# One column copied by VectorE in place of ScalarE at the end of a convolution's odd half

## The chip, the cores and the metric

The kernel runs on one core of a Trainium2 chip. The core has a matrix engine (TensorE, PE in the profile), a vector engine (VectorE, DVE), a scalar engine (ScalarE, ACT), a third elementwise engine (GpSimd, POOL) and a queue engine that mainly issues DMAs (SyncE, SP); ACT issues some DMAs too. Each engine works through its own list of instructions in order. An instruction that needs another engine's result, or a DMA's, waits at the head of its list, and everything behind it on that engine waits with it.

The metric is the device time of one execution in microseconds (us). Lower is better.

## The reference

One block of a diffusion transformer, with 1024 latent tokens of width 1024 and 256 context tokens. A combined projection feeds a Conformer convolution branch and a grouped-query attention branch; the two are gated, added and projected again. All arithmetic is float32. What matters here is the convolution: 31 taps, each of the 1024 channels by itself.

```
def conv_module(u, gate, conv_w, conv_b, ln_g, ln_b, w_conv_out):
    a, g = jnp.split(u, 2, axis=-1)
    y = a * jax.nn.sigmoid(g)
    pad = CONV_KERNEL // 2
    y = lax.conv_general_dilated(
        y, conv_w[:, None, :], window_strides=(1,), padding=[(pad, pad)],
        dimension_numbers=('NWC', 'WIO', 'NWC'), feature_group_count=CONV_WIDTH) + conv_b
    y = jax.nn.silu(layer_norm(y, ln_g, ln_b))
    y = y * jax.nn.silu(gate)
    return y @ w_conv_out
```

## The kernel before

The 1024 channels of the convolution are done in eight blocks of 128 (j = 0 to 7), one after the other. A channel lies on a partition and the tokens lie along the row. The input of a block is split into even tokens (`E`, 512 columns) and odd tokens (`O`, 512 columns), both in one tile `y`; the two running sums lie in a PSUM tile of two banks, which the profile calls `pconv`. There is only one such tile, so a block starts only when the one ahead of it is done.

`conv_taps` puts the steps of a block on a list `taps` as small functions. `pump` takes the next ones from that list and issues them, between the matmuls of the projections (`filler`), which run at the same time. In order a block is: `first` (two ACT instructions fill the two sums), 15 taps on VectorE into the even sum, `even_end` (POOL adds `E` and `O`), 15 taps into the odd sum, `odd_end`, `evens`, `turn`, 15 more taps, and `last`, whose VectorE instruction is the last reader of `pconv`; POOL then adds the block's output to `ysum`, and SP stores it (`accD`).

`odd_end` is the place of the change. A VectorE instruction writes columns 0 to 510 of `O` from the input one column to the right and the odd sum. Column 511 has no neighbour to its right, and so it is copied from the odd sum by itself (line 809). `evens` begins with a small reduction of `edge` and then reads `O`, so its first large instruction (line 817) stands behind that copy.

After the eighth block the kernel gives the PSUM banks of the convolution to the attention (`unshare(2)`, `share({"o": 1})`, `share({"s": 5})`). The first matmuls of the attention, those of `max_pieces`, which find the row maxima of the scores, write tiles `ps` in these banks. VectorE reduces each to a maximum (`mx`).

The projections go through a stream of jobs (`stream`, `wparts`, `proj`): a weight half is loaded by SP (`wraw`), cast on ACT to its high part (`whi`), and subtracted on POOL or VectorE to its low part (`wlo`). 24 matmuls (`ppj`) make one half of a job, after which ACT empties the bank (`ts`). While the flag `held` is set, the instructions of VectorE, ACT, POOL and PE stay in the order of the program text; it is cleared for VectorE, ACT and POOL once the projections of queries, keys and values are issued, while the eighth block is still under way, and from there a scheduler orders these engines' lists (`urgent()` raises an instruction's priority in it). Helpers record all instructions on line 50, so the profile tells them apart by tile names, not by lines.

Of the kernel before, what the change touches and what calls it, by code (L numbers as in the profile page):

```python
# [34 lines left out]
def block_kernel(ctx: ExitStack, tc: tile.TileContext, x, cx, cc, wmod, bmodT, bmodg, vecs, gpost,  # L35
# [18 lines left out]
    PE, V, S, G = (Ordered(e) for e in (nc.tensor, nc.vector, nc.scalar, nc.gpsimd))  # L54
# [11 lines left out]
    def tl(tag, shape, bufs, dtype=F32, pool="sb"):  # L66
        return pools[pool].tile(list(shape), dtype, tag=tag, bufs=bufs, name=nm(tag))
# [13 lines left out]
    def share(bufs):  # L81
        p = tc.tile_pool(name=nm("share"), bufs=1, space=PSUM, reuse_waits="tile")
        shares.append((p, p.__enter__(), bufs))

    def unshare(n):
        for _ in range(n):
            shares.pop()[0].__exit__(None, None, None)

    def pt(tag, shape=(P, 512), dtype=F32):
        if not any(tag in bufs for _, _, bufs in shares):  # L90
            tag = "s"
        for _, pool, bufs in shares:
            if tag in bufs:
                return pool.tile(list(shape), dtype, tag=tag, bufs=bufs[tag], name=nm("p" + tag))
# [685 lines left out]
    def conv_taps(j, y):  # L780
        st = {}
        E, O = y[:, 0, :], y[:, 1, :]

        def first():
            if j == 0:
                unshare(1)
                share({"conv": 1})
            st["acc"] = pt("conv", (P, 2, 512))
            S.activation(st["acc"][:, 1, :], O, AF.Identity, scale=cw[:, j, 14:15])
            S.activation(st["acc"][:, 0, :], E, AF.Identity, scale=cw[:, j, 15:16])  # L790

        def even_end():

            G.tensor_tensor(out=E, in0=E, in1=O, op=ALU.add)
            st["edge"] = tl("edge", (P, 10), 2)

        def tap(c, src, k, w):
            o = k - 7
            a, b = max(0, -o), min(512, 512 - o)
            acc = st["acc"][:, c, a:b]  # L800
            V.scalar_tensor_tensor(out=acc, in0=src[:, a + o:b + o], scalar=w, in1=acc, op0=ALU.mult, op1=ALU.add)

        def odd_end():

            acc = st["acc"]
            V.tensor_tensor(out=st["edge"][:, 0:8], in0=O[:, 0:8], in1=cw[:, j, 16:31:2], op=ALU.mult)
            V.scalar_tensor_tensor(out=O[:, 0:511], in0=O[:, 1:512], scalar=cw[:, j, 16:17], in1=acc[:, 1, 0:511],
                                   op0=ALU.mult, op1=ALU.add)
            S.copy(O[:, 511:512], acc[:, 1, 511:512])

        def evens():
            acc = st["acc"]
            st["out"] = tl("acc", (P, T), 2)
            out = st["out"][:].rearrange("p (u r) -> p r u", r=2)
            edge = st["edge"]
            V.tensor_reduce(out=edge[:, 8:9], in_=edge[:, 0:8], axis=AX.X, op=ALU.add)
            V.scalar_tensor_tensor(out=out[:, 0, 1:512], in0=acc[:, 0, 1:512], scalar=cvb[:, j:j + 1],
                                   in1=O[:, 0:511], op0=ALU.add, op1=ALU.add)
            V.scalar_tensor_tensor(out=out[:, 0, 0:1], in0=acc[:, 0, 0:1], scalar=cvb[:, j:j + 1], in1=edge[:, 8:9],
                                   op0=ALU.add, op1=ALU.add)  # L820

        def turn():
            acc = st["acc"]
            V.scalar_tensor_tensor(out=acc[:, 0, :], in0=acc[:, 0, :], scalar=ncvb[:, j:j + 1], in1=O,
                                   op0=ALU.add, op1=ALU.add)

        def last():
            acc = st["acc"]
            out = st["out"]
            V.scalar_tensor_tensor(out=out[:].rearrange("p (u r) -> p r u", r=2)[:, 1, :], in0=E,  # L830
                                   scalar=cs[:, j, 16:17], in1=acc[:, 0, :], op0=ALU.mult, op1=ALU.subtract)
            if j == 0:
                G.tensor_copy(ysum[:], out[:])
            else:
                G.tensor_tensor(out=ysum[:], in0=ysum[:], in1=out[:], op=ALU.add)
            SP.dma_start(out=accD[j][:], in_=out[:])

        ks = [k for k in range(16) if k != 7]
        taps.append(first)
        taps.extend(lambda k=k: tap(0, E, k, cw[:, j, 2 * k + 1:2 * k + 2]) for k in ks[:-1])  # L840
        taps.append(lambda: (even_end(), tap(1, O, 0, cw[:, j, 0:1])))
        taps.extend(lambda k=k: tap(1, O, k, cw[:, j, 2 * k:2 * k + 1]) for k in ks[1:] if k != 8)
        taps.append(odd_end)
        taps.append(evens)
        taps.append(turn)
        taps.extend(lambda k=k: tap(0, E, k, cs[:, j, k:k + 1]) for k in ks)
        taps.append(last)
# [775 lines left out]
```

## Time and profile before

| what | value |
|---|---|
| median of 3 runs | 1400.5 us (1398.6 to 1407.2) |
| the profiled execution | 1406.56 us |
| its span, first to last instruction | 1404.8 us |
| PE busy | 1353.0 us, 96% of the span |
| DVE busy | 1022.3 us, 73% |
| POOL busy | 712.5 us, 51% |
| ACT busy | 564.3 us, 40% |

The convolution's taps run on DVE from 76 to 571 us of the span, beside the projections on PE; the attention follows, from 563 us on. All times in rows of the profile are us from the start of the span. In a row of the timeline the first number is the start, the second the duration, and the bracket at the end tells how long the engine had been idle before it and what ended that. In a row of the waits the numbers are the sum, the count and the longest. In a row of the windows the busy time of each engine stands with the number of instructions, then the clock granted to PE as a share of full speed, the busy share of the DMA engines and their GB/s.

### The profile page before, as it was taken

To read this page: it belongs to the slowest core of one execution; us is meant where nothing else is said; L and a number is where in the kernel's file an instruction comes from. 1 tells how busy PE (TensorE), PEld (TensorE's weight loads), DVE (VectorE), ACT (ScalarE), POOL (GpSimd) and SP (SyncE) were. 2 spreads that over 40 slices of the span, in tenths; PEclk is the share of its full clock that TensorE was granted. 3 is DMA by queue.
4 is the path that set the end of the run, shared out by engine and by line. 5 is a ranking of instruction groups with operands and counts; after the bars stand their busy time and mean duration, and the time that the engine had idled before them with its cause. 6 is when DMAs were issued, how large, how long until landed. Compare 5 with 4: busy or idle time off the path is not lost.

```text
span 1404.8 us, 19526 instructions
## 1 busy us (share of the span) xinstructions
PE 1353.0 (96%) x6520; PEld 1003.3 (71%) x6520; DVE 1022.3 (73%) x1513; ACT 564.3 (40%) x1397; POOL 712.5 (51%) x577
## 2 busy tenths in 40 slices
PE   5999999999999999799999999999999999999996
PEld 3767898988889888566666666566666565788874
DVE  3477988897989896757766676677676676349967
ACT  5542344435343432145444444454454444222332
POOL 1121346567666552256764655565456666263623
PEclk9999999999999999899999999999999999999998
DMA  9731533544534448414554444544365567699754
GB/s 320 266 124 46 184 119 131 191 133 141 176 125 156 140 159 224 143 61 140 176 166 121 136 145 141 165 136 153 97 191 163 209 213 259 204 317 341 257 182 153
DMA packets 153332, 242.45 MB, mean 173 GB/s; under 512 B 19936, under 2 KB 72716, under 8 KB 153232
## 3 DMA queue, kind: packets, MB, share of 16 engines
q1 hardware_dynamic: 139792, 218.07, 47.4%
q10 hardware_dynamic: 13440, 23.14, 5.8%
q8 instruction: 51, 0.84, 0.3%
q14 instruction: 49, 0.40, 0.1%
HBM read 161.50 MB, written 79.52 MB: 172 GB/s over the span
## 4 chain that ended last, share of the span: by engine, by line
PE 76%; DVE 9%; DMA 4%; ACT 3%; POOL 3%; issue 3%; ACTq 0%; SPq 0%; POOLq 0%; DVEq 0%
PE ppj L50 34%; PE po L50 21%; PE ps L50 17%; PE pm L50 4%; DVE pconv L50 3%; DVE t L50 2%; DMA wm<-in_wmod 1%; DVE mx L50 1%; DMA y<-in_wout 1%; ACT pe L50 1%; POOL y L50 1%; POOL wgl L50 1%; DMA r<-r1D 1%; ACTq L50 0%; DVE acc L50 0%
## 5 line engine op out<-in xcount | busy, mean ns | idle before, releaser
L50 PE MATMUL ppj<-t,whi 128*128 128x512 f32 x1728 | 617.7, 402 | 4.6 <-DVE t L50 2.6
L50 PEld LDWEIGHTS ppj<-t,whi 128*128 128x128 f32 x1728 | 328.1, 190 | 107.7 <-issue 33.7
L50 PE MATMUL ppj<-t,wlo 128*128 128x512 f32 x864 | 341.8, 396 | 0.7 <-POOL wlo L50 0.7
L50 DVE TENSOR_REDUCE mx<-ps 128x1 f32<-128x512 f32 (+1 forms) x320 | 199.5, 681 | 105.3 <-PE ps L50 104.8
L50 ACT ACTIVATE pe<-ps 128x512 f32<-128x512 f32 x320 | 187.9, 597 | 205.1 <-PE ps L50 188.0
L50 PE MATMUL ps<-r,kk 128*128 128x512 f32 (+1 forms) x640 | 202.8, 398 | 0.4 <-DMA r<-mr 0.3
L50 POOL TENSOR_TENSOR psum<-psum,pe 128x512 f32<-128x512 f32 x128 | 173.9, 1375 | 41.9 <-ACT pe L50 38.1
L50 PEld LDWEIGHTS ppj<-t,wlo 128*128 128x128 f32 x864 | 164.8, 191 | 31.5 <-POOL wlo L50 1.8
L50 DVE SCALAR_TENSOR_TENSOR pconv<-y,cw,pconv 128x507 f32<-128x507 f32 (+5 forms) x224 | 168.0, 750 | 19.6 <-ACT pconv L50 13.4
L50 POOL TENSOR_TENSOR wlo<-wraw,whi 128x512 fp32r<-128x512 f32 x69 | 91.3, 1331 | 138.2 <-ACT whi L50 90.3
L50 PE MATMUL po<-pe,vt 128*64 128x512 f32 x640 | 144.4, 597 | 0.0
L50 PEld LDWEIGHTS ps<-r,kk 128*128 128x128 f32 (+1 forms) x640 | 121.3, 190 | 30.1 <-DMA r<-mr 0.7
L50 POOL TENSOR_TENSOR psum<-psum,part 128x512 f32<-128x512 f32 x64 | 89.1, 1394 | 105.1 <-DVE part L50 105.1
L50 PE MATMUL po<-wgh,t 128*128 128x384 f32 x512 | 131.7, 338 | 0.0
L50 PEld LDWEIGHTS po<-pe,vt 128*64 128x64 f32 x640 | 43.1, 136 | 81.2 <-issue 79.2
L50 PEld LDWEIGHTS po<-wgh,t 128*128 128x128 f32 x512 | 92.9, 188 | 1.3
L50 DVE SCALAR_TENSOR_TENSOR pconv<-y,cs,pconv 128x505 f32<-128x505 f32 (+7 forms) x120 | 90.0, 750 | 3.6
L50 PE MATMUL po<-wgl,t 128*128 128x384 f32 x256 | 86.3, 337 | 0.0
L50 ACT CAST whi<-wraw 128x512 fp32r<-128x512 f32 x112 | 69.1, 630 | 37.4 <-DMA wraw<-in_wch 17.7
L50 POOL TENSOR_TENSOR psum<-pe,pe 128x512 f32<-128x512 f32 x32 | 42.4, 1344 | 75.0 <-ACT pe L50 75.0
L50 PE MATMUL ps<-kk,rq 64*128 64x512 f32 (+1 forms) x384 | 66.5, 406 | 13.8 <-DVE acc L50 7.4
L50 DVE TENSOR_TENSOR part<-pe,pe 128x512 f32<-128x512 f32 x64 | 68.2, 1068 | 13.6 <-ACT pe L50 13.5
(221 smaller groups left out, 1808.3 us busy)
## 6 DMA issues: line engine op xcount, KB each, us to landing
wraw<-in_wch SPq DMA_DIRECT2D x96, 256.0 KB
opD<-opw SPq DMA_DIRECT2D x56, 256.0 KB
wm<-in_wmod SPq DMA_DIRECT2D x24, 512.0 KB
W<-opD SPq DMA_DIRECT2D x48, 256.0 KB
r1D<-r1st SPq DMA_DIRECT2D x32, 256.0 KB
y<-accD SPq DMA_DIRECT2D x16, 512.0 KB
r<-r1D ACTq DMA_DIRECT2D x32, 256.0 KB
opD<-acc SPq DMA_DIRECT2D x13, 512.0 KB
```

The lines of the kernel that those rows point to most:

```text
L50: i = f(*a, **k)
```

## The change

The copy of column 511 is issued on VectorE (`V.tensor_copy`) in place of ScalarE (`S.copy`). It is executed once for each of the eight blocks; source (PSUM), destination (SBUF) and values are the same.

```
@@ -806,7 +806,7 @@
             V.tensor_tensor(out=st["edge"][:, 0:8], in0=O[:, 0:8], in1=cw[:, j, 16:31:2], op=ALU.mult)
             V.scalar_tensor_tensor(out=O[:, 0:511], in0=O[:, 1:512], scalar=cw[:, j, 16:17], in1=acc[:, 1, 0:511],
                                    op0=ALU.mult, op1=ALU.add)
-            S.copy(O[:, 511:512], acc[:, 1, 511:512])
+            V.tensor_copy(O[:, 511:512], acc[:, 1, 511:512])
 
         def evens():
             acc = st["acc"]
```

The order of the instructions at the eighth block shows what moves. On VectorE the copy stands between the instruction that writes columns 0 to 510 of `O` and the first of `evens`, which writes `acc_5777` (the eighth block's output; `pconv_5512` is its pair of sums, `y_1048_4996` its `E` and `O`):

```order
 L50 SCALAR_TENSOR_TENSOR pconv_5512<-y_1048_4996,cw,pconv_5512 128x504
 L50 SCALAR_TENSOR_TENSOR y_1048_4996<-y_1048_4996,cw,pconv_5512 128x511
+L50 COPY y_1048_4996<-pconv_5512 128x1
 L50 SCALAR_TENSOR_TENSOR acc_5777<-pconv_5512,vec,y_1048_4996 128x511
 L50 SCALAR_TENSOR_TENSOR acc_5777<-pconv_5512,vec,edge_5614 128x1
```

One row came in, and no other row moved on VectorE here.

On ScalarE the copy stood behind the cast of a projection weight (`whi_5872`) and the emptying of a projection's bank (`ts_5833`), and ahead of a DMA that loads a gate of the attention:

```order
 L50 ACTIVATE ts_5833<-ppj_5803 128x512
 L50 CAST whi_5872<-wraw_5839 128x512
-L50 COPY y_1048_4996<-pconv_5512 128x1
 L50 DMA gate_6245<-gbD_697 128x512
 L50 ACTIVATE ts_5879<-ppj_5841 128x512
```

One row went out; the others keep their order. In the other seven blocks the two engines change in the same way, and in the seventh two reductions of `edge` also change places on VectorE.

On SP, behind the eighth block, two transfers of 512 KB move up: the load of the first block's output for the layer norm (`y_1383_6595`) by two places, and the store of the eighth block's output (`accD_664`) by one.

```order
 L149 DMA wraw_6042<-in_wch 128x512
+L1059 DMA y_1383_6595<-accD_659 128x1024
 L853 DMA tgbD_685<-ts_5912 128x512
+L836 DMA accD_664<-acc_5777 128x1024
 L149 DMA wraw_6044<-in_wch 128x512
-L1059 DMA y_1383_6595<-accD_659 128x1024
-L836 DMA accD_664<-acc_5777 128x1024
 L853 DMA tgbD_686<-ts_5973 128x512
```

Both now stand ahead of the weight load `wraw_6044`, and the layer-norm load ahead of the store of a projection's half (`tgbD_685`) as well. Earlier on SP one weight load (`wraw_3403`) moves ahead of three stores, and on POOL the addition of the eighth block to `ysum` moves ahead of one `wlo`. The list of PE is the same.

More of the change, by code (lines that the diff above doesn't have):

```diff
@@ L808, in odd_end @@
                                    op0=ALU.mult, op1=ALU.add)
-            S.copy(O[:, 511:512], acc[:, 1, 511:512])
+            V.tensor_copy(O[:, 511:512], acc[:, 1, 511:512])
         def evens():
```

## The prediction

> **What bounds the kernel now.** I looked first for stretches in which PE, busy for 96% of the span, is not busy. Windows of 20 us over the whole span show one such stretch at the place of the change, where the convolution ends and the attention begins:
>
> ```profile
> 520.00:540.00 20.00, 20.00 (x93) 16.55 (x93) 19.27 (x28) 6.28 (x12) 8.46 (x8) 1.00 0.74 235
> 540.00:560.00 20.00, 19.63 (x87) 15.92 (x86) 8.98 (x13) 2.99 (x6) 3.21 (x3) 1.00 1.02 247
> 560.00:580.00 20.00, 12.59 (x46) 8.86 (x45) 15.53 (x23) 2.33 (x4) 4.92 (x3) 0.74 0.71 205
> ```
>
> The columns behind the length are PE, PE's weight loads, DVE, ACT, POOL, PE's granted clock, the busy share of the DMA engines and GB/s. PE is full until 560 and then loses 7.4 of 20 us, with a clock of 0.74. One window earlier DVE, full before, falls to 8.98: the gap on DVE comes first. DMA is at its limit there (1.02). The waits between 535 and 585 us name both gaps:
>
> ```profile
> DVE acc L50 <- ACT y L50: 10.6, 1, 10.6
> ...
> PEld ps L50 <- DVE acc L50: 7.7, 1, 7.7
> PE ps L50 <- DVE acc L50: 7.4, 1, 7.4
> ```
>
> `ACT y` is the copy of column 511 and `DVE acc` is the first instruction of `evens` in the first row, and the instruction of `last` in the other two. The timeline of DVE shows the eighth block from `odd_end` (545.46) on:
>
> ```profile
> 545.46 0.75 DVE L50 SCALAR_TENSOR_TENSOR y<-y,cw,pconv 128x511 f32<-128x511 f32 x1
> 556.80 0.75 DVE L50 SCALAR_TENSOR_TENSOR acc<-pconv,vec,y 128x511 f32<-128x511 f32 x1 [10.59 <-ACT y L50]
> ...
> 570.31 0.75 DVE L50 SCALAR_TENSOR_TENSOR acc<-y,cs,pconv 128x512 f32<-128x512 f32 x1
> ```
>
> The copy's input was ready at 546.21, and DVE went on at 556.80. The timeline of ACT says where the copy was meanwhile:
>
> ```profile
> 550.59 0.62 ACT L50 CAST whi<-wraw 128x512 fp32r<-128x512 f32 x1 [4.92 <-DMA r<-r1D]
> 550.62 3.49 ACTq L50 DMA_DIRECT2D r<-r1D  x3
> 554.16 0.60 ACT L50 ACTIVATE ts<-ppj 128x512 f32<-128x512 f32 x1 [2.95 <-DMA vt<-vD]
> 556.09 0.62 ACT L50 CAST whi<-wraw 128x512 fp32r<-128x512 f32 x1 [1.33 <-DMA wraw<-in_wch]
> ...
> 556.61 0.15 ACT L50 COPY y<-pconv 128x1 f32<-128x1 f32 x1
> ```
>
> It stood behind casts and DMA issues of the projections and the attention, each of which waited for a transfer. So a copy of 0.15 us, unrelated to those transfers, made DVE wait for them, and the convolution's end came at 570.31 + 0.76 = 571.07. PE shows what that held up:
>
> ```profile
> 563.21 0.49 PE L50 MATMUL ps<-kk,rq 64*128 64x512 f32 x1
> 571.11 1.22 PE L50 MATMUL ps<-kk,rq 64*128 64x512 f32 x3 [7.41 <-DVE acc L50]
> ```
>
> The second matmul of the row maxima needs the bank that `last` reads. It started 0.04 us after that instruction ended.
>
> **The change part by part.** First, what goes: the wait of DVE at the eighth block. With the copy on DVE, `evens` starts at 546.21 plus the copy, not at 556.80. No row shows a copy of one column on DVE; the nearest rows are these groups by shape, after the ACT copy itself (busy time and mean of one in ns, then the idle time before them):
>
> ```profile
> L50 ACT COPY y<-pconv 128x1 f32<-128x1 f32 x8 | 1.3, 164 | 18.3 <-DVE y L50 11.6 <-DVE edge L50 6.7
> L50 DVE SCALAR_TENSOR_TENSOR acc<-pconv,vec,edge 128x1 f32<-128x1 f32 x8 | 1.7, 209 | 0.0
> L50 DVE TENSOR_REDUCE edge<-edge 128x1 f32<-128x8 f32 x8 | 1.1, 151 | 0.0
> ```
>
> One DVE instruction on one column takes 0.15 us without PSUM and 0.21 us with it. I take 0.21, since the copy reads PSUM, and 0.03 us of issue, 0.24 together. A copy that overlaps its neighbours could cost nothing. From `evens` to the end of `last` DVE took 571.07 - 556.80 = 14.27 us with no further wait, so the eighth block should end at 546.21 + 0.24 + 14.27 = 560.7. PE asks for the bank at 563.4, 2.7 us later. So PE would not wait for VectorE here at all, and 2.7 us is the cover that hides the copy; if it were gone, every microsecond beyond it would be PE's.
>
> Second, what PE gains. The matmuls of the row maxima are pipelined, so the time from the first to the end of the wait counts, not only the 7.4 us in which PE was wholly empty; the weight-load row gives 7.7 us. Then the clock. Windows of 2 us show it low in the gap and behind it:
>
> ```profile
> 566.00:568.00 2.00, 0.00 (x0) 0.00 (x0) 1.89 (x4) 0.55 (x1) 1.27 (x1) 0.50 0.96 328
> ...
> 574.00:576.00 2.00, 2.00 (x6) 1.55 (x6) 0.00 (x0) 0.00 (x0) 0.00 (x0) 0.57 0.89 363
> 576.00:578.00 2.00, 2.00 (x10) 1.15 (x9) 0.65 (x2) 0.60 (x1) 0.00 (x0) 1.00 0.10 41
> ```
>
> [...] The chain of waits prices it, with the same work once at half and once at full clock:
>
> ```profile
> 571.11 1.22 PE ps L50 x3
> 572.33 4.56 PE ppj L50 x12
> 576.89 0.66 PE ps L50 x4
> 577.55 2.93 PE ppj L50 x12
> ```
>
> Three of four `ps` at full clock are 0.50 us, so the slow pieces cost (1.22 - 0.50) + (4.56 - 2.93) = 2.35 us. Without the gap the clock should stay at 1.00. PE's gain is 7.7 + 2.35 = 10.05 us.
>
> Third, the other seven blocks. The first row is from the waits over the whole span, the others are PE's longest from 60 to 562 us:
>
> ```profile
> DVE acc L50 <- ACT y L50: 11.4, 6, 10.6
> ```
>
> ```profile
> PE po L50 <- DVE x L50: 1.8, 2, 1.3
> PE ppj L50 <- DVE ts L50: 1.6, 1, 1.6
> PE pm L50 <- DMA wm<-in_wmod: 1.2, 2, 0.9
> PE ppj L50 <- POOL wlo L50: 0.7, 2, 0.4
> PE ppj L50 <- ACT ts L50: 0.4, 1, 0.4
> ```
>
> Seven blocks lose only 11.4 - 10.6 = 0.8 us of waits and gain up to 7 x 0.24 = 1.7 us of copies on DVE, 0.9 us more work over 480 us. Only waits for DVE could feel it, and PE's projections hide it: PE has 20.00 of 20 us busy at 520 to 540, though DVE has 19.27. I cost it at nothing. ACT no longer stands idle for VectorE (18.3 us over eight copies), so what is queued behind the copy can start sooner; PE's waits for ACT and for POOL's `wlo`, which follows ACT's casts, are 0.4 + 0.7 = 1.1 us in all, so up to 1.1 us could be gained, and again I take nothing. The one weight load on SP that moves ahead of three stores falls under the same bound, as only `wlo` hangs on it.
>
> [...]
>
> Fourth, the queues. The layer-norm load and, behind it, the store of the eighth block waited on SP for `last`, and so did the addition on POOL; these are the timelines of SP and of POOL:
>
> ```profile
> 563.43 0.33 SPq L149 DMA_DIRECT2D wraw<-in_wch  x1
> ...
> 571.09 0.32 SPq L1059 DMA_DIRECT2D y<-accD  x1
> ```
>
> ```profile
> 571.14 2.36 POOL L50 TENSOR_TENSOR ysum<-ysum,acc 128x1024 f32<-128x1024 f32 x1 [3.25 <-DVE acc L50]
> ```
>
> With `last` ending at 560.7, SP, which issues the weight load ahead of it at 563.43, reaches the layer-norm load with its wait already over, so nothing behind it is held. The 1 MB of both transfers, however, moves from a free stretch into the full one before 568. At the 328 GB/s of the window at 566 that is 1.05 MB / 328 GB/s = 3.2 us of delay for weight loads behind it. They serve a projection job after the next, so I cost it at nothing, with 3.2 us as the other end. The addition's 2.36 us fall into POOL's idle time.
>
> **The sum.** Against the profiled execution: 1406.56 - 10.05 = 1396.5 us, of which the span would be 1394.8 (1.8 us lie around it before). That execution is 6.1 us above the median of 1400.5, so the forecast for the median is 1400.5 - 10.05 = **1390.4 us**. It supposes that the wait is as long without the profiler.
>
> **The rivals.**
> - *The transfers collide.* The 1 MB that moves up delays a weight half that PE soon needs. For it: DMA shares of 1.02 in the window at 540 and 0.96 in that at 566. Against: weights are cast a job ahead. 1390.4 + 3.2 = 1393.6.
> - *The clock's part comes back.* PE reaches the row maxima faster than VectorE reduces them, and waits for banks. Price 2.35, so 1392.8. Against it: DVE is busy for only 0.65 of 2.00 us in the window at 576, where both engines work on the maxima.
> - *Slower: the wait belongs to the profiled execution alone.* Only because transfers were late was ACT late at the copy. If in the timed runs `wraw` lands some 10.5 us earlier, ACT is at the copy when its input is ready (546.21), DVE never waits, and the change only adds: 8 x 0.24 - 0.8 = 1.1 us where VectorE bounds, 1401.6. It decides from a landing about 7.7 us earlier, where PE's wait is already gone. For it: the profiled execution is 6.1 us slower than the median, and runs differ by 8.6. Against it: four transfers in a row held ACT, in a stretch with DMA at 1.02, which the bytes demand and not an accident. [...]
>
> **How the numbers follow.** Forecast 0.66; transfers 0.10; clock 0.08; slower 0.11; 0.05 for what I don't see. The forecast's own range is half of the runs' spread of 8.6, 4.3 us, to either side: 1386 to 1395. The two smaller gains reach from there to 1398, with noise 1399. The range 1386 to 1399 leaves out the slower case and part of the tails, about 2 in 10. One per cent, about what a measurement of this kernel can tell from no change, is 14.0 us: faster means below 1386.5, slower above 1414.5. The forecast is 0.7%, so most of it lies within; 0.10 is for faster (the forecast's lower edge), 0.87 for the same, 0.03 for slower.
>
> **What would show it.** In the profile after: no wait of DVE for `ACT y`, the last `acc` near 561, `ps` matmuls running on from 563 with the clock at 1.00 through 564 to 578, PE near 20 of 20 in the window at 560, and a span near 1395. A copy on DVE well over 0.24 us would show the cost wrong. PE idle behind 563 with another name as the releaser would show a wait in place of the old one, and a span gain well above 10 a hold of ACT that I cost at nothing.

## The result, and the profile after

The kernel after takes 1392.06 us (median of 7 runs, 1391.61 to 1395.87); beside it, on the same chips, the kernel before took 1405.21 us (7 runs, 1398.60 to 1407.22). The ratio is 0.9924, with a 95% interval of 0.9906 to 0.9943: 10.7 us less, 8 to 13 us by the interval. (The medians lie 13.2 us apart, the means, 1403.9 and 1393.2, 10.8.) That is 0.76%, less than the 1% at which the prediction draws the line between same and faster, but clearly shorter. The profiled execution took 1392.78 us, its span 1391.0 us.

First the windows of the kernel after at the place of the change (columns as before: PE, PE's weight loads, DVE, ACT, POOL, granted clock, DMA share, GB/s):

```profile
540.00:560.00 20.00, 19.82 (x88) 16.10 (x87) 17.55 (x26) 2.94 (x5) 2.59 (x2) 1.00 1.04 252
560.00:580.00 20.00, 19.90 (x93) 12.99 (x91) 14.19 (x24) 4.28 (x8) 7.50 (x5) 1.00 0.72 235
```

PE is full through both, at full clock; before, the second had 12.59 us of PE at a clock of 0.74. DVE has 17.55 us of work in the window at 540 in place of 8.98.

The timeline of DVE in the kernel after, at the eighth block:

```profile
543.34 0.75 DVE L50 SCALAR_TENSOR_TENSOR y<-y,cw,pconv 128x511 f32<-128x511 f32 x1
544.12 0.16 DVE L50 COPY y<-pconv 128x1 f32<-128x1 f32 x1
544.19 0.74 DVE L50 SCALAR_TENSOR_TENSOR acc<-pconv,vec,y 128x511 f32<-128x511 f32 x1
...
557.69 0.75 DVE L50 SCALAR_TENSOR_TENSOR acc<-y,cs,pconv 128x512 f32<-128x512 f32 x1
```

`evens` now starts 0.07 us behind the start of the copy, and `last` ends at 558.44. The copies as a group (shortest, mean and longest in ns, then the first and the last start):

```profile
L50 DVE COPY y<-pconv x8: 157/158/160, 125.8 to 544.1; 128x1 f32<-128x1 f32 x8
```

The timeline of PE after, and that of ACT in the same stretch:

```profile
560.85 0.73 PE L50 MATMUL ps<-kk,rq 64*128 64x512 f32 x4
564.44 0.73 PE L50 MATMUL ps<-kk,rq 64*128 64x512 f32 x4
```

```profile
548.48 0.62 ACT L50 CAST whi<-wraw 128x512 fp32r<-128x512 f32 x1 [4.57 <-DMA r<-r1D]
...
553.77 0.62 ACT L50 CAST whi<-wraw 128x512 fp32r<-128x512 f32 x1 [1.36 <-DMA wraw<-in_wch]
```

The first four `ps` matmuls, of which three came 7.41 us behind the first, are now one group without a gap. ACT is still held by the same transfers, 4.57 us at the DMA issues of `r` and 1.36 us at `wraw`, but nothing of the eighth block stands behind them any more.

Four events cut a span into parts: the first tap of the convolution on DVE, the first `ps` on PE, the start of `mr` on ACT (the first instruction after the row maxima), and the end. The rows of before and of after:

```profile
75.92 0.75 DVE L50 SCALAR_TENSOR_TENSOR pconv<-y,cw,pconv 128x505 f32<-128x505 f32 x1 [1.14 <-ACT pconv L50]
...
591.79 0.27 ACT L50 ACTIVATE mr<-ps 8x128 fp32r<-8x128 f32 x1 [6.49 <-PE ps L50]
```

```profile
73.81 0.75 DVE L50 SCALAR_TENSOR_TENSOR pconv<-y,cw,pconv 128x505 f32<-128x505 f32 x1 [1.14 <-ACT pconv L50]
...
579.37 0.27 ACT L50 ACTIVATE mr<-ps 8x128 fp32r<-8x128 f32 x1 [6.44 <-DMA rq<-r1D]
```

With the first `ps` at 563.21 and 560.85 and the spans of 1404.8 and 1391.0 this gives the first two lines of the table, in us. The others are the profiled executions of the experiments below, read in the same way.

| kernel | to the first tap | tap to first `ps` | first `ps` to `mr` | `mr` to the end | span |
|---|---|---|---|---|---|
| before | 75.92 | 487.29 | **28.58** | 813.0 | 1404.8 |
| after | 73.81 | 487.04 | **18.52** | 811.6 | 1391.0 |
| on VectorE in the eighth block alone | 72.52 | 488.05 | **18.52** | 813.2 | 1392.3 |
| on VectorE in all but the eighth | 72.62 | 486.61 | **28.18** | 812.8 | 1400.2 |
| on ScalarE, earlier in its list | 76.19 | 487.11 | **18.53** | 815.0 | 1396.8 |
| after, 3 added copies | 75.35 | 486.44 | **18.55** | 809.4 | 1389.7 |
| after, 8 added copies | 74.81 | 484.20 | **23.62** | 809.9 | 1392.5 |
| after, 14 added copies | 72.78 | 484.56 | **29.30** | 817.5 | 1404.1 |
| after, 2 added in each of the first seven | 74.05 | 492.21 | **18.52** | 806.2 | 1391.0 |

Of the 13.8 us between the spans of before and after, 10.06 lie between the first `ps` and `mr`. 2.1 us lie ahead of the first tap, some 50 us before the first of the copies is executed, and 1.4 behind `mr`. The other lines show that these outer parts differ from one profiled execution to the next (72.5 to 76.2 and 806.2 to 817.5 us) without regard to the copy, while the five kernels without PE's wait have 18.52 to 18.55 us in the section. The stretch from the first tap to the first `ps` is 486.4 to 488.1 us in six of the nine. The two shorter ones (8 and 14 added copies) are ahead long before the eighth block: in the 40 us behind the first tap PE does 219 and 217 matmuls there, 202 to 210 in the others. The longer one is taken up below. So the section tells the kernels apart, and a single total does not: it can be off by some 10 us that have nothing to do with the copy.

### The profile page after: what moved, and what is told of

The parts are those of the page before. It is cut to its first block, busy times and chain, and to the rows that moved or that the text cites. A ratio compares the mean times of both kernels' runs of the same rounds, so it can differ in the third digit from the quotient of the medians.

```text
span 1391.0 us, 19520 instructions
## 1 busy us (share of the span) xinstructions
PE 1347.2 (97%) x6520; PEld 999.8 (72%) x6520; DVE 1018.9 (73%) x1521; ACT 564.6 (41%) x1389; POOL 712.7 (51%) x577
## 4 chain that ended last, share of the span: by engine, by line
PE 79%; DVE 6%; DMA 5%; ACT 4%; POOL 3%; issue 2%; ACTq 1%; SPq 0%; POOLq 0%; DVEq 0%
PE ppj L50 37%; PE po L50 21%; PE ps L50 17%; PE pm L50 4%; DVE t L50 2%; DMA wm<-in_wmod 1%; ACT pe L50 1%; DVE pconv L50 1%; POOL y L50 1%; DVE mx L50 1%; DMA y<-in_wout 1%; POOL wgl L50 1%; DMA vt<-vD 1%; ACTq L50 1%; ACT ts L50 0%
## 5 line engine op out<-in xcount | busy, mean ns | idle before, releaser
L50 DVE TENSOR_TENSOR part<-pe,pe 128x512 f32<-128x512 f32 x64 | 68.4, 1072 | 14.5 <-ACT pe L50 10.6
```

What stands on the lines that cost most here:

```text
L50: i = f(*a, **k)
```

## The experiments

### One block, and the other seven

The theory: the whole gain is the wait in the eighth block. The rival: freeing ScalarE from the copy in the other blocks, or the copies' own price there, has a part in it. Two kernels split the change. In the first:

```diff
-            S.copy(O[:, 511:512], acc[:, 1, 511:512])
+            (V.tensor_copy if j == KD - 1 else S.copy)(O[:, 511:512], acc[:, 1, 511:512])
```

> The copy is on VectorE in the eighth block alone; the first seven blocks keep it on ScalarE. Theory (the whole gain is the wait at the eighth block): the same gain as the change, 10 us below the kernel before at the wait itself (1391 to 1395 us), DVE without a wait before evens of the eighth block, PE running on through the row maxima. Rival (the gain is spread: ScalarE is set free eight times, 18.3 us of ScalarE's idle time): at most an eighth to a half of the gain, 1 to 6 us.

Measured: 1396.0 us (5 runs, 1391.32 to 1398.96), ratio to before 0.9931 (0.9903 to 0.9959). The median is 1 us above the 1391 to 1395 expected, the gain by the ratio, 9.7 us, is the expected one. The section takes 18.52 us, the same as after to the hundredth. In the second kernel the two engines are exchanged:

```diff
-            S.copy(O[:, 511:512], acc[:, 1, 511:512])
+            (S.copy if j == KD - 1 else V.tensor_copy)(O[:, 511:512], acc[:, 1, 511:512])
```

> The copy is on VectorE in blocks one to seven and stays on ScalarE in the eighth. Theory: no gain, within 2 us of the kernel before; DVE waits about 10.6 us for ScalarE at the eighth block, PE about 7.4 us for the bank, the clock falls to 0.50. Rival (freeing ScalarE in the earlier blocks matters): half of the gain or more, 5 to 10 us.

Measured: 1403.5 us (10 runs, 1400.72 to 1410.46), ratio 1.0006 (0.9980 to 1.0033): no gain. The timelines of ACT, DVE and PE in this kernel have the old picture:

```profile
552.51 0.15 ACT L50 COPY y<-pconv 128x1 f32<-128x1 f32 x1
```

```profile
552.70 0.75 DVE L50 SCALAR_TENSOR_TENSOR acc<-pconv,vec,y 128x511 f32<-128x511 f32 x1 [10.78 <-DMA r<-r1D]
```

```profile
559.23 0.49 PE L50 MATMUL ps<-kk,rq 64*128 64x512 f32 x1
567.01 1.22 PE L50 MATMUL ps<-kk,rq 64*128 64x512 f32 x3 [7.29 <-DVE acc L50]
```

DVE waits for 10.78 us and goes on 0.04 us after the copy's end at 552.66. The name behind the wait, a DMA, is an inference from the semaphores and misses the last link; the row of ACT shows it.

What follows: the gain is the eighth block's, within what the intervals can tell. Seven copies more or fewer on either engine change nothing that these runs can see.

### The engine, or the place in its list?

The theory: ScalarE is not too slow for the copy; the copy stands too late in ScalarE's list. Then it may stay there, if it stands ahead of the instructions that wait for transfers. The rival: an exchange between engines costs something by itself, so that only a copy on VectorE removes the wait. In this kernel the scheduler gives the copy precedence; in the eighth block it moves ahead of two casts `whi`, two `ts` and the DMA issues between them:

```diff
-            S.copy(O[:, 511:512], acc[:, 1, 511:512])
+            with urgent():
+                S.copy(O[:, 511:512], acc[:, 1, 511:512])
```

> The copy stays on ScalarE in all blocks, but is raised in priority, which at the eighth block puts it ahead of the emptying of a projection's bank and of two weight casts in ScalarE's list; in the first seven blocks the order is kept. Theory (it is the place in the queue that counts, not the engine): ScalarE reaches the copy at about 545 us, waits about 1 us for VectorE, and DVE goes on at about 546.5; most of the gain, 8 to 10 us. What is behind the copy on ScalarE comes up to 1.5 us later, which could cost PE at most that. Rival (VectorE must do it because ScalarE is held by DMA issues ahead of the copy as well): DVE still waits several us, and the gain is 5 us or less.

Measured: 1395.62 us (median of 7 runs, 1390.25 to 1398.60), ratio 0.9934 (0.9906 to 0.9961). An eighth run took 5311.77 us, for which nothing on record gives a reason; it is in neither figure (with it, the median is 1396.62). ACT and DVE in this kernel:

```profile
544.16 0.46 ACTq L50 DMA_DIRECT2D rq<-r1D  x1
546.26 0.16 ACT L50 COPY y<-pconv 128x1 f32<-128x1 f32 x1 [6.99 <-DVE y L50]
```

```profile
545.48 0.75 DVE L50 SCALAR_TENSOR_TENSOR y<-y,cw,pconv 128x511 f32<-128x511 f32 x1
546.46 0.75 DVE L50 SCALAR_TENSOR_TENSOR acc<-pconv,vec,y 128x511 f32<-128x511 f32 x1 [0.23 <-ACT y L50]
```

Now ScalarE waits for the copy's input, and VectorE for 0.23 us in place of 10.59. ACT's idle time of 6.99 us is mostly not the copy's: its issue queue is held up to 544.62, so the copy keeps ACT for at most 546.26 - 544.62 = 1.64 us. The section takes 18.53 us, as with the copy on VectorE.

What follows: the place in the queue decides, not the engine. The exchange costs 0.23 us against the 0.07 us of the copy on VectorE, and the cover hides both.

### Where the cover ends

The theory has a second half: VectorE may end the eighth block up to 2.7 us later at no cost, and beyond that PE pays, with the clock's part on top. The rival: the wait of PE belongs to something else that the change happened to move, such as the transfers on SP; then a delay that is put back on VectorE would not bring back the time. These kernels add copies of 512 columns behind the copy of column 511 in the eighth block (3, 8 or 14 of them; they overwrite the odd sum after its last use):

```diff
             V.tensor_copy(O[:, 511:512], acc[:, 1, 511:512])
+            for _ in range(14 if j == KD - 1 else 0):
+                V.tensor_copy(acc[:, 1, :], O)
```

> The change, with 14 copies of 128x512 on VectorE between odd_end and evens of the eighth block, into the odd sum, which nobody reads any more; they stand in for the old wait of 10.6 us without touching ScalarE. At about 0.7 to 0.78 us each, 9.8 to 10.9 us. Theory (2.6 us of cover, then every us is PE's, then the half clock): PE waits 7.2 to 8.3 us at the row maxima, the clock falls to 0.50 and costs about 2.35 us more; the time is that of the kernel before within 2 us, 9.5 to 10.7 above the change. Rival (the gain came from something on ScalarE, and VectorE's delay is absorbed): less than 5 us above the change.

> The change, with 3 copies of 128x512 into the unread odd sum on VectorE at the eighth block: 3 x 0.73 = 2.2 us of delay. Theory (2.6 us of cover at the eighth block): last ends about 0.4 us before PE asks for the bank, PE does not wait, the stretch from the first ps matmul of the row maxima to the maxima's rows on ScalarE is the 18.5 us of the change (it was 28.6 before). Rival (no cover, every us of VectorE at the eighth block is PE's): 2 us longer.

> The change, with 8 such copies, 8 x 0.73 = 5.8 us of delay. Theory: PE waits 5.8 - 2.6 = 3.2 us for last; the same stretch takes 3.2 us more, and up to 2.35 more if the clock falls in a gap that short, 21.7 to 24.1 us. Rival (delay is PE's in full): 5.8 us or more of wait, above 24.3 us.

With 14 copies: 1404.65 us (10 runs, 1398.49 to 1408.32), ratio to before 0.9994 (0.9974 to 1.0014). That is the time of the kernel before, as expected; above the change it is 12.6 us by the medians, more than the 9.5 to 10.7 expected. DVE and PE:

```profile
540.79 10.17 DVE L50 COPY pconv<-y 128x512 f32<-128x512 f32 x14
```

```profile
565.31 1.22 PE L50 MATMUL ps<-kk,rq 64*128 64x512 f32 x3 [7.47 <-DVE acc L50]
```

With 8, one profiled execution: 1394.32 us (1404.23 for before beside it):

```profile
542.38 5.80 DVE L50 COPY pconv<-y 128x512 f32<-128x512 f32 x8
```

```profile
559.01 0.49 PE L50 MATMUL ps<-kk,rq 64*128 64x512 f32 x1
562.53 0.92 PE L50 MATMUL ps<-kk,rq 64*128 64x512 f32 x3 [3.02 <-DVE acc L50]
```

With 3, one profiled execution: 1391.49 us:

```profile
545.29 2.15 DVE L50 COPY pconv<-y 128x512 f32<-128x512 f32 x3
560.99 0.75 DVE L50 SCALAR_TENSOR_TENSOR acc<-y,cs,pconv 128x512 f32<-128x512 f32 x1
```

```profile
561.79 0.73 PE L50 MATMUL ps<-kk,rq 64*128 64x512 f32 x4
```

A delay of 2.15 us costs nothing in the section (18.55 us), though `last` ends only 0.05 us before the first `ps`. 5.80 us cost 23.62 - 18.52 = 5.10 us, and 10.17 us cost 10.78. So 10.17 us of plain work on VectorE, with the copy still on VectorE, bring back the time of the kernel before. What follows: PE's wait hangs on the end of `last`. In all four kernels that have the wait, PE goes on 0.05 to 0.06 us after it (with 8 copies `last` runs from 561.73 to 562.48, with 14 from 564.50 to 565.25). The loss begins between 2.15 and 5.80 us of delay, as a cover of 2.6 to 2.7 us demands. The transfers on SP are also put off when `last` is late, so these kernels alone do not part the two. But with 3 copies both transfers stand behind the store of a projection's half (`tgbD` at 563.36, `y` at 563.83, `accD` at 564.26), where the kernel after has the layer-norm load ahead of it, and the section is the same. The two kernels with one execution each support this by their sections, not by their totals.

### Time to spare in the first seven blocks?

The prediction costed 0.9 us of more work on VectorE over seven blocks at nothing. Is that because VectorE has time to spare there, or because 0.9 us is little? Two added copies in each of the first seven blocks make it 10.2 us:

```diff
             V.tensor_copy(O[:, 511:512], acc[:, 1, 511:512])
+            for _ in range(2 if j < KD - 1 else 0):
+                V.tensor_copy(acc[:, 1, :], O)
```

> The change, with 2 such copies in each of the first seven blocks, 14 x 0.73 = 10.2 us of additional work on VectorE, none at the eighth. Theory (the first seven blocks have VectorE time to spare, so copies there cost nothing): PE stays at 20 of 20 us from 160 to 540, odd_end of the eighth block comes at most 2.6 us later against the first ps matmul, and PE waits less than 0.5 us; the stretch from the first ps matmul to the maxima's rows stays at 18.5 us. Rival (VectorE is a queue without slack, and what is added anywhere comes out at its end): last ends 10 us later, PE waits about 7.5 us there, and the stretch takes 28 us.

Measured in one profiled execution: 1392.84 us, span 1391.0, the same as after. The section takes 18.52 us, and `last` ends at 563.50, 2.8 us before the first `ps` at 566.26. So the rival, by which the work comes out at the end of the eighth block, falls. But the table shows that this equality is made of two differences: the stretch from the first tap to the first `ps` took 492.21 us, against 484.20 to 488.05 in all others, and the tail was the shortest, 806.2 us. PE falls behind most in the first block; these are its windows, first of the kernel after and then of this one:

```profile
120.00:140.00 20.00, 18.47 (x83) 14.81 (x83) 18.56 (x32) 3.72 (x8) 6.13 (x5) 1.00 0.32 92
140.00:160.00 20.00, 20.00 (x101) 18.00 (x100) 17.76 (x24) 8.72 (x30) 4.57 (x3) 1.00 0.77 246
```

```profile
120.00:140.00 20.00, 17.21 (x77) 13.53 (x76) 18.57 (x32) 3.72 (x8) 6.22 (x5) 1.00 0.24 68
140.00:160.00 20.00, 20.00 (x90) 17.39 (x90) 17.45 (x24) 7.92 (x21) 4.52 (x3) 0.91 0.86 271
```

PE loses 1.26 us in the first window and runs at a clock of 0.91 in the second, where it does 90 matmuls in place of 101. Its waits there, and the only one of the kernel after in the same stretch:

```profile
132.19 0.50 PE L50 MATMUL ppj<-t,whi 128*128 128x512 f32 x1 [0.97 <-DVE y L50]
139.74 0.50 PE L50 MATMUL ppj<-t,whi 128*128 128x512 f32 x1 [1.82 <-DVE ts L50]
```

```profile
138.13 0.50 PE L50 MATMUL ppj<-t,whi 128*128 128x512 f32 x1 [1.53 <-DVE ts L50]
```

So the wait for `ts` is mostly an old one, and what is new is 0.97 + (1.82 - 1.53) = 1.26 us. The lower clock costs, as an estimate from the two windows, 0.09 x 20 = 1.8 us more. The other 2 us of the 5.2 come later, in waits for ScalarE: 0.50 us for `qk` at 450.43, and this one for `ts`, which is 0.18 us in the kernel after:

```profile
557.87 0.50 PE L50 MATMUL ppj<-t,whi 128*128 128x512 f32 x1 [1.64 <-ACT ts L50]
```

What follows: "time to spare" holds only in part. From 120 to 140 us VectorE is busy for 18.57 of 20 us and PE hangs on it, and ten times the work does reach PE there, by some 3 us with the clock's part. Whether the copies have a part in the waits for ScalarE too, one execution doesn't show. For the change itself, 0.9 us over the seven blocks, nothing is visible: 487.04 us from the first tap to the first `ps` after, 487.29 before. The short tail goes with the clock granted there, as the last section shows beside the longest one; that the added copies have no part in it was not tried.

## Why the prediction was right

**The time.** 1390.4 us were forecast, 1392.06 measured, inside the range of 1386 to 1399 and inside the likeliest case's own 1386 to 1395. The mechanism and the step's size were nearer than the total: 10.05 us forecast for PE, 10.06 us found between the first `ps` and `mr`. By parts that is 7.41 us of empty PE, 2.3 us of half clock and 0.35 us around them (the last section shows how), against the 7.7 and 2.35 forecast; that the sums agree to 0.01 us is chance. The totals agree to 1.7 us by luck as well: the base was 4.7 us too low (1400.5 forecast from, 1405.21 measured) and the medians' difference 3.1 us above 10.05 (13.15). The ratios of the three kernels that lose the wait, 0.9924, 0.9931 and 0.9934, are 9.3 to 10.7 us and lie around 10.05. The median of 1400.5 came from three runs; 24 further executions of the kernel before, beside the experiments, have a median of 1405.6 (1396.58 to 1409.41). The profiled execution of 1406.56 was thus an ordinary one, and the sum against it (1396.5) and the sum against the median of three lie on either side of the result.

**The wait that goes.** `last` was to end 2.7 us before PE asks for the bank. After, it ends at 558.44, and PE's second `ps`, 0.2 us behind the first at 560.85 (563.4 behind 563.21 before), at about 561.0: 2.6 us. The runs with 3 and 8 added copies bracket this cover.

**The copy.** 0.24 us were taken, with 0 as the other end. It is 0.158 us long and overlaps its successor: 0.07 us from start to start. By the program text `evens` reads columns 0 to 510 of `O` only; the reader of column 511 is `turn`, behind it. Where the next instruction does read column 511, as the first of 3 added copies does, it starts 0.19 us after the copy (545.29 behind 545.10). With the copy on ScalarE, `evens` waited for it all the same; why, no run here shows. The row of `edge`, 0.209 us, was the wrong neighbour, the reduction of 0.151 us the right one; the 0.03 us of issue are what the timeline of before shows between two instructions of VectorE (one from 557.71 to 558.47, the next from 558.50). The copy itself is about as long on either engine: 158 ns on VectorE after, 164 ns on ScalarE before. What made it dear on ScalarE was the queue: VectorE waited 10.59 us for it at the eighth block.

**The other seven blocks** were costed at nothing, and the two kernels that split the change agree. That ACT might gain up to 1.1 us was left out, rightly: with seven copies taken off it the stretch up to the first `ps` is 486.61 us, among the 486.4 to 488.1 of the others, and the total does not move.

**A sign that misled.** "A span gain well above 10" was to show a hold of ACT. The gain was 13.8, and it is no such hold, since its surplus lies ahead of the first tap and behind `mr`. The sign ought to have been the section's time and not the span.

**The rivals.** *The transfers collide*: these are the issues on SP after, with both transfers ahead of the weight load at 566.27, and, from the waits from 535 to 585 us, those of PE for the reductions, for transfers and for casts:

```profile
562.51 0.38 SPq L1059 DMA_DIRECT2D y<-accD  x1
562.99 0.38 SPq L853 DMA_DIRECT2D tgbD<-ts  x1
563.42 0.42 SPq L836 DMA_DIRECT2D accD<-acc  x1
566.27 0.33 SPq L149 DMA_DIRECT2D wraw<-in_wch  x1
```

```profile
PEld ps L50 <- DVE mx L50: 0.8, 2, 0.4
PEld ps L50 <- DMA r<-mr: 0.7, 1, 0.7
...
PEld ppj L50 <- ACT whi L50: 0.4, 1, 0.4
PE ps L50 <- DMA r<-mr: 0.3, 1, 0.3
```

No projection waits for a weight transfer, and what waits for a cast is a weight load of 0.4 us, so the 3.2 us did not come. *The clock's part comes back*: PE's wait for banks is the 0.8 us of `DVE mx`, on weight loads, and the section is shorter by the full 10.06. *The wait belongs to the profiled execution alone*: no. With the copy back on ScalarE in the eighth block alone, DVE waited 10.78 us in a profiled execution of its own, and ten runs agreed with before; nor was any of the 24 times of before (1396.58 at the lowest) near 1390.

## What to carry to other kernels

An instruction on an in-order queue inherits every wait that stands ahead of it, however small it is: 0.15 us of copying cost this kernel 10 us (a section of 28.58 us against 18.52), because it stood behind casts and DMA issues that waited for transfers. A small step between two instructions of one engine is better placed on that engine, or ahead of the waiting instructions; here both removed the wait. How much of a wait the kernel gets back can be told beforehand: it is what the consumer itself waited, and the time between the end of the freed work and the moment at which its consumer asks is the cover, the delay that still costs nothing (here 2.6 of 10.6 us). Where the total wanders by more than the effect, measure the stretch between two events on either side of it.

## What the runs showed of the clock

The 2.35 us taken for the half clock hold for one execution. Finer windows of four kernels show when the half clock begins and ends (the granted clock is the third number from the end). Before:

```profile
565.00:565.50 0.50, 0.00 (x0) 0.00 (x0) 0.50 (x1) 0.00 (x0) 0.00 (x0) 0.98 0.92 243
...
575.50:576.00 0.50, 0.50 (x3) 0.43 (x2) 0.00 (x0) 0.00 (x0) 0.00 (x0) 0.78 0.85 336
```

All but the eighth block on VectorE:

```profile
564.00:564.40 0.40, 0.00 (x0) 0.00 (x0) 0.40 (x1) 0.00 (x0) 0.00 (x0) 0.84 0.70 123
...
570.80:571.20 0.40, 0.40 (x2) 0.30 (x1) 0.00 (x0) 0.00 (x0) 0.00 (x0) 0.62 1.05 430
```

14 added copies:

```profile
560.80:561.20 0.40, 0.00 (x0) 0.00 (x0) 0.40 (x1) 0.00 (x0) 0.40 (x1) 0.91 0.86 333
...
571.00:571.40 0.40, 0.40 (x3) 0.22 (x1) 0.00 (x0) 0.00 (x0) 0.00 (x0) 0.54 0.07 31
```

8 added copies:

```profile
562.80:563.20 0.40, 0.40 (x3) 0.02 (x1) 0.40 (x2) 0.00 (x0) 0.40 (x1) 0.62 0.84 323
...
566.00:566.40 0.40, 0.40 (x2) 0.30 (x2) 0.00 (x0) 0.00 (x0) 0.00 (x0) 0.61 1.23 72
```

The windows next to these show only 1.00 on one side and 0.50 on the other. So a mean of 0.98 over 0.50 us is half clock for (1 - 0.98) / 0.5 x 0.50 = 0.02 us, and the clock fell at 565.48; the other edges come out in the same way. PE's gap is taken from its rows; the cost is half of the time in which PE worked at half clock.

| kernel | PE empty | clock falls | clock back | at half | half of PE's time at half clock | section above 18.52 |
|---|---|---|---|---|---|---|
| before | 563.70 to 571.11 | 565.48 | 575.72 | 10.24 | 2.3 | 10.06 |
| all but the eighth | 559.72 to 567.01 | 564.27 | 571.10 | 6.83 | 2.0 | 9.66 |
| 14 added | 557.84 to 565.31 | 561.13 | 571.37 | 10.24 | 3.0 | 10.78 |
| 8 added | 559.51 to 562.53 | 562.90 | 566.31 | 3.41 | 1.7 | 5.10 |

The times at half clock, 3.41, 6.83, 10.24 and 10.24 us, are 1, 2, 3 and 3 times the shortest of them, wherever PE's gap lies. In each kernel the section's excess is the gap plus the clock's part plus 0.3 to 0.4 us (before: 7.41 + 2.3 + 0.35). So the clock's part was 1.7 to 3.0 us for these gaps, and the prediction's 2.35 fitted because it was read from the very execution that it was subtracted from; that every execution of the kernel before pays as much is not shown.

What sets these times, the four executions don't show. The clock fell 1.78 us after PE's last matmul in the kernel before, 4.55 us after it in the kernel with all but the eighth block on VectorE and 3.29 us after it with 14 copies; with 8 copies PE was empty for 3.02 us only, and the clock fell 0.37 us after PE had gone on. It came back, in the order of the table, 4.61, 4.09, 6.06 and 3.78 us after PE had gone on. The length of the gap alone does not give the time at half clock: gaps of 7.29 to 7.47 us went with 6.83 us in one execution and 10.24 in two.

Not expected either was how far the parts around the section differ between executions: 3.7 us ahead of the first tap and 11.3 us behind `mr`, over nine profiled executions. The tail's difference shows in the clock. These are windows of 100 us, 400 and 500 us behind `mr`, of the execution with the longest tail (14 added copies) and of that with the shortest (2 added in each of the first seven blocks):

```profile
986.64:1086.64 100.00, 97.09 (x443) 61.19 (x443) 65.34 (x100) 45.45 (x84) 52.51 (x40) 0.97 0.50 156
1086.64:1186.64 100.00, 96.34 (x453) 60.53 (x453) 65.48 (x86) 43.36 (x80) 62.42 (x46) 0.97 0.65 219
```

```profile
984.78:1084.78 100.00, 98.95 (x480) 60.80 (x477) 68.06 (x105) 46.92 (x87) 52.39 (x40) 1.00 0.55 177
1084.78:1184.78 100.00, 96.32 (x450) 61.85 (x449) 68.43 (x84) 44.73 (x81) 70.21 (x50) 1.00 0.64 220
```

The slower tail has a clock of 0.97 in both, the faster one 1.00, and in the first the slower did 443 matmuls in place of 480. Over the 24 executions of before the time falls by 1.4 us for each 0.001 of the mean granted clock (a line fitted to time and clock, correlation -0.91), and 0.001 of some 1400 us is 1.4 us. So most of the spread goes with the granted clock. Why one execution is granted less than another was not tried.
